# Two hybrid diffusion layers on one core: the feed-forward's GpSimd work moved to VectorE, modulation and sums of squares to TensorE

## The chip, the core and the metric

The kernel runs on one NeuronCore of a Trainium2 chip. The core has a matmul engine (TensorE, PE in the views, its weight loads PEld), a vector engine (VectorE, DVE), an activation engine (ScalarE, ACT), a general engine (GpSimd, POOL) and a queue that issues the loads here (SyncE, SP). The metric is the device time of one execution in microseconds; less is better.

## What is computed

Two layers run on 512 latent tokens and 256 context tokens of width 1024. Each layer is a half-step SwiGLU feed-forward, a mixer of four head groups, and a second half-step SwiGLU. Every block is preceded by an RMS norm and a modulation whose shift, scale and gate come from a conditioning vector through a matrix of 1024 x 9216 per layer. The lines that matter here are these:

```python
def rms_norm(x, g):
    y = xf * lax.rsqrt(jnp.mean(xf * xf, -1, keepdims=True) + RMS_EPS)
def modulate(h, shift, scale):
    return h * (1.0 + scale) + shift
def swiglu(h, w_in, w_out):
    u = h @ w_in
    return (jax.nn.silu(u[..., :D_FF]) * u[..., D_FF:]) @ w_out
...
    mod = (jax.nn.silu(c) @ w_mod[l] + b_mod[l]).reshape(c.shape[0], N_MOD, 1, D_MODEL)
    mod_c = (jax.nn.silu(c_ctx) @ w_mod[l] + b_mod[l]).reshape(N_MOD, 1, D_MODEL)
    x = x + 0.5 * mod[:, 2] * swiglu(modulate(rms_norm(x, norm_g[l, 0]), mod[:, 0], mod[:, 1]), ffn_w_in[l, 0], ffn_w_out[l, 0])
```

D_FF is 2816, that is 22 blocks of 128. All data are float32. The last feed-forward runs on the latent tokens alone.

## The kernel before

**Stages.** The program is six stages in a row: feed-forward 1 of layer 0, mixer 0, feed-forward 2 of layer 0, feed-forward 1 of layer 1, mixer 1, feed-forward 2 of layer 1. They are called FF1, mixer, FF2, FF3, mixer, FF4 below. Activations are kept transposed, features on partitions: `xT` is eight tiles of 128 features x 768 tokens.

**One block of a feed-forward.** `up` makes the 128 gate and 128 value features of one block from seven products in place of eight: tokens are cut in two halves of 384 (256 in FF4), the 1024 input features in even and odd tiles of 128, and the products EVEN1, T1, T2, ODD1, T3, ODD2, T4 are taken of sums and differences of these, on the side of the tokens (made once per stage, by `pair_even` and `pair_odd`) and on the side of the weights (made per block, by `w1_operands`). Every operand is split in two fp32r parts, high and low: ScalarE writes the high part (L440), VectorE the low part (L441). A product is four pairs of feature tiles times three matmuls (high x high, high x low, low x high), so a block is 84 matmuls of 384 or 386 columns (`ul`, L484). Banks of PSUM carry running sums from product to product; ScalarE copies some out (`pc`), VectorE adds some (L489), and the next product on that bank waits for these.

After `up`, three multiplications with the tokens' 1/rms (`rsb`, L526), the bias columns `ub`, silu, the gating (L539) and another split (L543, L544) give the block's hidden features. Two or three blocks are a chunk (CK); after a chunk the down-projection `y` adds its share to `xT`: 8 output tiles x blocks x 3 matmuls x 2 token segments (L428, L430, L432), then one VectorE operation per segment (L563).

**GpSimd's part.** L455 makes four weight combinations of 128x512 per block on GpSimd (`w1s`, `w1r`), and two of the three multiplications with `rsb` (L526) are GpSimd's too. So are two differences per pair in `pair_odd` (L378, L382).

**Modulation.** A block of the modulation is 512 of its columns. Four blocks are made at the start by `mod_direct` (L203: eight float32 matmuls with 32 output rows each, into four column groups of the array; L205 copies the sums out, L208 turns them into columns). The other 32 (14 in FF1, 6 in FF2, 12 in FF3) are made in the background by `mod_block`: eight loads of 128x512, and VectorE multiplies and adds them one by one into `macc` (L225, L227), once per conditioning vector; `mod_sum` adds over partitions with small matmuls (L242, L248).

**Sums of squares.** For the next norm, ScalarE squares each `xT` tile (L270), VectorE adds the squares up in `ss` (L271), and six small matmuls sum over partitions at the end (L297).

**Order.** The program is written in Tile: a scheduler orders the instructions of each engine by priorities (order of writing, shifted by `high_priority`) and by what its own model finds ready; LATER = 300 puts background work last. Every engine, the load queue too, then runs in that fixed order.

## Time and profile before

| | us |
|---|---|
| median of three runs | 3644.53 |
| the three runs | 3642.72, 3644.53, 3649.85 |
| the profiled execution | 3636.23 |
| its span, first to last instruction | 3634.4 |
| FF1 (its start in front: 76.9) | 628.9 |
| FF2 / FF3 / FF4 | 543.9 / 566.8 / 397.5 |
| mixers | 722.2 / 597.5 |

Stages are stretches of the one profiled execution, cut at the first product of each feed-forward's second block and at the last down-projection. Busy times of TensorE count overlapping matmuls once. Idle time is what is left of a stretch. A line of the view of groups has the line of the kernel, engine, operation, tiles out<-in, form, count, then busy time and mean duration, then the idle time ahead of it on its engine and who ended it.

### The profile page before, as it was taken

What the parts mean: (1) busy time and instruction counts of PE and PEld (TensorE: products, weight loads), DVE (VectorE), ACT (ScalarE), POOL (GpSimd) and SP (SyncE); (2) the same over time, 40 slices, a digit from 0 to 9 for tenths busy, and PEclk for the clock granted to TensorE, in tenths of its full rate; (3) what the DMA queues carried; (4) which work ended last, traced back from release to release, by engine and by line L of the source; (5) the groups of instructions that cost most, each with busy time, mean ns of one, the idle gap of its engine ahead of it and who ended that gap; (6) DMA issues with size and microseconds to landing.
All of it is one profiled execution on the core that took longest, in us unless ns stands there. A gap on an engine that the chain in (4) does not pass through costs nothing. (4 is left out here: it accounts for less than half of the span.)

```text
span 3634.4 us, 59477 instructions
## 1 busy us (share of the span) xinstructions
PE 3304.8 (91%) x22788; PEld 2804.5 (77%) x22788; DVE 2680.1 (74%) x5306; ACT 1496.4 (41%) x3168; POOL 1010.8 (28%) x910
## 2 busy tenths in 40 slices
PE   6898998899998997999999799999999989978887
PEld 5787788787775665888998788989888766567886
DVE  7898888645548867777776887777555578687776
ACT  5232333322447743333334433333423567443443
POOL 2343333100003212434442424433000023143442
PEclk9999999999999998999999899999999989999999
DMA  6333333211100002232221333333212100132221
GB/s 208 110 99 100 112 105 105 62 44 45 41 14 1 11 22 88 85 93 85 87 81 42 113 102 114 104 99 113 61 47 54 31 1 15 39 90 90 82 90 58
DMA packets 332941, 267.69 MB, mean 74 GB/s; under 512 B 33748, under 2 KB 281712, under 8 KB 332656
## 3 DMA queue, kind: packets, MB, share of 16 engines
q1 hardware_dynamic: 332656, 263.89, 24.4%
q8 instruction: 179, 2.93, 0.3%
q14 instruction: 106, 0.87, 0.1%
HBM read 261.73 MB, written 2.10 MB: 73 GB/s over the span
## 5 line engine op out<-in xcount | busy, mean ns | idle before, releaser
L484 PE MATMUL ul<-bh,w1h 128*128 128x386 f32 (+3 forms) x2464 | 833.3, 338 | 115.0 <-DVE sg L489 66.0
L484 PE MATMUL ul<-bh,w1l 128*128 128x386 f32 (+3 forms) x2464 | 816.9, 332 | 1.1 <-DVE w1l L441 1.0
L484 PE MATMUL ul<-bl,w1h 128*128 128x386 f32 (+3 forms) x2464 | 816.3, 331 | 0.0
L484 PEld LDWEIGHTS ul<-bh,w1h 128*128 128x128 f32 x2464 | 478.9, 194 | 157.8 <-DVE sg L489 72.0
L440 ACT ACTIVATE w1h<-w1r 128x512 fp32r<-128x512 f32 x528 | 329.9, 631 | 546.2 <-PE ul L484 311.0
L441 DVE TENSOR_TENSOR w1l<-w1r,w1h 128x512 fp32r<-128x512 f32 x528 | 441.3, 839 | 82.6 <-ACT w1h L440 81.7
L484 PEld LDWEIGHTS ul<-bh,w1l 128*128 128x128 f32 x2464 | 477.9, 194 | 9.7 <-issue 6.9
L484 PEld LDWEIGHTS ul<-bl,w1h 128*128 128x128 f32 x2464 | 479.7, 195 | 3.1 <-issue 2.9
L227 DVE SCALAR_TENSOR_TENSOR macc<-wm,sc,macc 128x512 f32<-128x512 f32 x392 | 414.2, 1076 | 7.0 <-DMA wm<-in_w_mod_dram 6.6
L563 DVE SCALAR_TENSOR_TENSOR xT<-y,gate,xT 128x512 f32<-128x512 f32 x448 | 266.8, 630 | 167.2 <-PE y L432 166.8
L455 POOL TENSOR_TENSOR w1s<-w1r 128x512 f32<-128x512 f32 x88 | 137.1, 1558 | 908.3 <-DVE w1l L441 831.2
L432 PE MATMUL y<-gh,w2l 128*128 128x512 f32 x1232 | 349.7, 355 | 37.4 <-DVE w2l L441 37.3
L428 PE MATMUL y<-gh,w2h 128*128 128x512 f32 x1232 | 351.5, 355 | 13.0 <-ACT w2h L440 10.9
L430 PE MATMUL y<-gl,w2h 128*128 128x512 f32 x1232 | 347.4, 352 | 0.2 <-DVE gl L544 0.2
L455 POOL TENSOR_TENSOR w1r<-w1r 128x512 f32<-128x512 f32 x176 | 269.8, 1533 | 164.9 <-issue 108.1
L440 ACT ACTIVATE w2h<-wo 128x384 fp32r<-128x384 f32 (+1 forms) x256 | 124.3, 494 | 351.2 <-PE y L430 317.1
L432 PEld LDWEIGHTS y<-gh,w2l 128*128 128x128 f32 x1232 | 199.2, 193 | 78.3 <-DVE w2l L441 47.0
L428 PE MATMUL pj<-hh,pwh 128*128 128x512 f32 (+2 forms) x864 | 251.8, 342 | 3.3 <-DVE qA L1092 1.8
L432 PE MATMUL pj<-hh,pwl 128*128 128x512 f32 (+2 forms) x864 | 243.1, 336 | 1.5 <-DVE pwl L441 1.5
L430 PE MATMUL pj<-hl,pwh 128*128 128x512 f32 (+2 forms) x864 | 244.2, 337 | 0.0
L428 PEld LDWEIGHTS y<-gh,w2h 128*128 128x128 f32 x1232 | 201.7, 193 | 48.3 <-ACT w2h L440 15.5
L430 PEld LDWEIGHTS y<-gl,w2h 128*128 128x128 f32 x1232 | 199.9, 192 | 32.2 <-DVE gl L544 0.5
(383 smaller groups left out, 5628.7 us busy)
## 6 DMA issues: line engine op xcount, KB each, us to landing
w1r<-in_ffn_w_in_dram SPq DMA_DIRECT2D x352, 256.0 KB
wm<-in_w_mod_dram SPq DMA_DIRECT2D x288, 256.0 KB
wo<-in_ffn_w_out_dram SPq DMA_DIRECT2D x88, 512.0 KB
pw<-in_w_in_dram SPq DMA_DIRECT2D x46, 512.0 KB
pw<-in_w_in_dram SPq DMA_DIRECT2D x16, 256.0 KB
wo<-in_w_out_dram SPq DMA_DIRECT2D x128, 32.0 KB
wo<-in_w_out_dram SPq DMA_DIRECT2D x64, 64.0 KB
rtab<-in_k_rope_dram SPq DMA_DIRECT2D x4, 512.0 KB
```

Source lines behind the costliest of these rows:

```text
L227: eng.scalar_tensor_tensor(out=acc[v], in0=r, scalar=s, in1=acc[v], op0=ALU.mult, op1=ALU.add)
L428: nc.tensor.matmul(p, lhsT=wh, rhs=xh[:, o:o + n], start=first, stop=False)
L430: nc.tensor.matmul(p, lhsT=wh, rhs=xl[:, o:o + n], start=False, stop=False)
L432: nc.tensor.matmul(p, lhsT=wl, rhs=xh[:, o:o + n], start=False, stop=last)
L440: nc.scalar.activation(out=hi, in_=raw, func=AF.Copy)
L441: nc.vector.tensor_tensor(out=lo, in0=raw, in1=hi, op=ALU.subtract)
L455: tt = lambda out, x, y, op: nc.gpsimd.tensor_tensor(out=out, in0=x, in1=y, op=op)
L484: nc.tensor.matmul(out, lhsT=w[:, m, :], rhs=x[:, m, x0:], start=start and m == j == 0, stop=m == KT // 2 - 1 and j == 2, skip_group_check ...
L563: nc.vector.scalar_tensor_tensor(out=xs, in0=py[s], scalar=gt[s][:, n_:n_ + 1], in1=xs, op0=ALU.mult, op1=ALU.add)
```

## The change

The 32 background blocks of modulation are made by TensorE as at the start: `mod_load` loads half a block (four tiles `wm`, where two were kept), `mod_some` multiplies the half that is there (four float32 matmuls, 32 x 512, in four column groups) and loads the next; one half per feed-forward block, two while many are left. `mod_block` and `mod_sum` are gone, and with them L225, L227, L242 and L248.

The sums of squares are added by TensorE: six matmuls of one column (four where there are only latent tokens) for each of the eight tiles, into one bank; the additions L271 are gone.

GpSimd has nothing left in the feed-forwards: combinations, multiplications and differences are VectorE's, the two bias columns are ScalarE's.

`ready` makes the tokens' operands in the order in which the products take them: of each pair first EVEN1, T1 and T2, and the rest of all four pairs after the last tile, at lower priority (REST). At the start, the rest is made between the first block's products, and the weights of the first block are loaded ahead of two modulation blocks. The down-projection's weights of a chunk are loaded together, one block ahead of the chunk's last.

```diff
-    def mod_block(self, l, b):
-        for k in range(KT):
-            r = self.raw.tile([128, 512], F32, name="wm", tag="wm", bufs=2)
-            nc.sync.dma_start(out=r, in_=a["w_mod"][l, k * 128:(k + 1) * 128, b * 128:b * 128 + 512])
-            for v in vs:
-                s = self.sc[:, k, v:v + 1]
-                eng = nc.gpsimd if v and MODPOOL else nc.vector
-                if k == 0:
-                    eng.tensor_scalar(out=acc[v], in0=r, scalar1=s, scalar2=None, op0=ALU.mult)
-                else:
-                    eng.scalar_tensor_tensor(out=acc[v], in0=r, scalar=s, in1=acc[v], op0=ALU.mult, op1=ALU.add)
-        self.macc = l, b, vs, acc
...
-        pt = self.psum("modps", "ms")
-        for v in vs:
-            for h in range(2):
-                g = 2 * v + h
-                with self.tc.high_priority(offset=g):
-                    nc.tensor.matmul(pt[32 * g:32 * g + 32, :256], lhsT=self.ones1, rhs=acc[v][:, 256 * h:256 * h + 256], start=True, stop=True)
...
+    def mod_load(self):
+        self.mod_now = None
+        if self.mod_todo:
+            l, b, h = self.mod_now = self.mod_todo.pop(0)
+            self.mod_w = [self.raw.tile([128, 512], F32, name="wm", tag="wm", bufs=4) for _ in range(4)]
+            for k, r in enumerate(self.mod_w):
+                self.nc.sync.dma_start(out=r, in_=self.a["w_mod"][l, (4 * h + k) * 128:(4 * h + k + 1) * 128, b * 128:b * 128 + 512])
+    def mod_some(self, left):
+        nc = self.nc
+        for _ in range(2 if len(self.mod_todo) + 1 > left else 1):
+            if self.mod_now is None:
+                return
+            l, b, h = self.mod_now
+            if h == 0:
+                self.mod_ps = self.psum("modps", "ms")
+            for k, r in enumerate(self.mod_w):
+                with self.tc.high_priority(offset=k):
+                    nc.tensor.matmul(self.mod_ps[32 * k:32 * k + 32, :], lhsT=self.sc[:, 4 * h + k, :], rhs=r, start=h == 0, stop=h == 1,
+                                     skip_group_check=True)
+            if h == 1:
+                self.mod_rows(l, b, self.mod_ps)
+            self.mod_load()
...
-    def sumsq(self, k, segs=SEGS):
+    def sumsq(self, k, segs=SEGS, tag="ms"):
...
         n0, n1 = segs[0][0], segs[-1][0] + segs[-1][1]
         if k == 0:
-            self.ss = self.work.tile([128, T], F32, name="ss", tag="ss", bufs=1)
-            nc.scalar.activation(out=self.ss[:, n0:n1], in_=self.xT[k][:, n0:n1], func=AF.Square)
-            return
+            self.ssps = self.psum("ssps", tag)
         sq = self.work.tile([128, T], F32, name="sq", tag="t3")
         nc.scalar.activation(out=sq[:, n0:n1], in_=self.xT[k][:, n0:n1], func=AF.Square)
-        nc.vector.tensor_tensor(out=self.ss[:, n0:n1], in0=self.ss[:, n0:n1], in1=sq[:, n0:n1], op=ALU.add)
+        for b in range(n0 // 128, n1 // 128):
+            nc.tensor.matmul(self.ssps[:, b:b + 1], lhsT=sq[:, b * 128:(b + 1) * 128], rhs=self.mean, start=k == b == 0, stop=k == KT - 1,
+                             skip_group_check=True)
+        if k == KT - 1:
+            self.ss = self.work.tile([128, 8], F32, name="ssc", tag="ssc", bufs=1)[:, :n1 // 128]
+            nc.vector.tensor_copy(self.ss, self.ssps[:, :n1 // 128])
...
-    def pair_odd(self, m, segs, e2, o2, new):
+    def pair_odd(self, m, segs, e2, o2, t):
...
         ne, go = self.rg[-1][:, 2 * m:2 * m + 1], self.rg[0][:, 2 * m + 1:2 * m + 2]
         self.second(2 * m + 1, segs, o2)
         yield
-        t = new()
         nc.vector.scalar_tensor_tensor(out=t, in0=e, scalar=ne, in1=e2, op0=ALU.mult, op1=ALU.add)
         self.parts(T1, m, t)
         yield
-        nc.gpsimd.tensor_tensor(out=t, in0=o2, in1=t, op=ALU.subtract)
+        nc.vector.tensor_tensor(out=t, in0=o2, in1=t, op=ALU.subtract)
         self.parts(T2, m, t)
         yield
         self.parts(ODD1, m, o, go)
-        nc.gpsimd.tensor_tensor(out=e2, in0=o2, in1=e2, op=ALU.subtract)
+        yield
+        nc.vector.tensor_tensor(out=e2, in0=o2, in1=e2, op=ALU.subtract)
         self.parts(T3, m, e2)
         yield
         self.parts(ODD2, m, o2)
         self.parts(T4, m, t)
         yield
...
+                self.held, self.rest = [], []
+            with self.tc.high_priority(offset=-SQ1):
+                self.sumsq(k, segs, tag)
...
-            new = lambda tag="pc", bufs=NPC: self.tmp.tile([128, self.half], F32, name="x2", tag=tag, bufs=bufs)
+            m = k // 2
             if k % 2 == 0:
-                self.e2 = new("sg", 1)
-                self.pair_even(k // 2, segs, self.e2)
-            else:
-                for _ in self.pair_odd(k // 2, segs, self.e2, new(), new):
-                    pass
+                self.held.append([self.half_tile() for _ in range(3)])
+                self.pair_even(m, segs, self.held[m][0])
+                return
+            e2, o2, t = self.held[m]
+            self.rest.append(self.pair_odd(m, segs, e2, o2, t))
+            for _ in range(3):
+                next(self.rest[m])
+            if k == KT - 1:
+                for i in range(3):
+                    with self.tc.high_priority(offset=-REST - 15 * i):
+                        for c in self.rest:
+                            next(c)
...
-        tt = lambda out, x, y, op: nc.gpsimd.tensor_tensor(out=out, in0=x, in1=y, op=op)
+        tt = lambda out, x, y, op: nc.vector.tensor_tensor(out=out, in0=x, in1=y, op=op)
         yield cut(q[0, 0])
...
             wh, wl = next(ops)
+            if first and n != EVEN1:
+                for r in self.rest:
+                    next(r, None)
...
+        self.mod_todo = [(*t, h) for t in background for h in range(2)]
...
-            wo = self.raw.tile([128, cn, D], F32, name="wo", tag="wo", bufs=1)
...
-                nc.sync.dma_start(out=wo[:, j, :], in_=w2[l, i, ff * 128:(ff + 1) * 128, :])
...
                 mul(nc.vector, g[:, :H], p[:, 2:H + 2], self.rsb[:, :H])
-                mul(nc.gpsimd, g[:, H:], g[:, H:], self.rsb[:, H:])
-                mul(nc.gpsimd, t[:, 2:], t[:, 2:], self.rsb)
+                mul(nc.vector, g[:, H:], g[:, H:], self.rsb[:, H:])
+                mul(nc.vector, t[:, 2:], t[:, 2:], self.rsb)
...
-                    nc.vector.tensor_copy(b[:, 0, :], t[:, 0:2])
-                    nc.vector.tensor_copy(b[:, 1, :], p[:, 0:2])
+                    nc.scalar.copy(b[:, 0, :], t[:, 0:2])
+                    nc.scalar.copy(b[:, 1, :], p[:, 0:2])
...
-                self.mod_sum()
                 with self.tc.high_priority(offset=-LATER):
-                    background(ff)
+                    if ff:
+                        self.mod_some(DFF // 128 - ff)
+                    else:
+                        self.mod_load()
                 if ff < DFF // 128 - 1:
                     ahead = self.up(l, i, ff + 1, False)
+                if j == cn - 2:
+                    wo = self.raw.tile([128, cn, D], F32, name="wo", tag="wo", bufs=1)
+                    for q in range(cn):
+                        nc.sync.dma_start(out=wo[:, q, :], in_=w2[l, i, (f + q) * 128:(f + q + 1) * 128, :])
...
+            if ci == len(chunks) - 1:
+                if switch:
+                    switch()
+                else:
+                    self.held_open([(self.fw, "pc", NPC, 1), (self.fw, "sg", 1, 2), (self.raw, "wm", 4, 1), (self.work, "ss", 1, 2)])
...
         for b in (8, 12):
-            self.mod_direct(0, b, ring(self.hl, "w1h", 4, NW1) + ring(self.hl, "w1l", 4, NW1))
+            self.mod_direct(0, b, self.mod_pieces(0, b, ring(self.hl, "w1h", 4, NW1) + ring(self.hl, "w1l", 4, NW1)))
+        self.first_w1 = self.w1_load(0, 0, 0)
...
-        for _ in range(5):
-            for s in stages:
-                next(s)
-        for k in range(KT):
-            self.sumsq(k)
-        self.raw_rows(self.fw)
-        with self.tc.high_priority(offset=-SOON):
-            for b in (0, 4):
-                w = self.raw.tile([128, 6, 512], F32, name="wm6", tag="wo", bufs=1)
-                self.mod_direct(0, b, [w[:, i, :] for i in range(6)] + ring(self.raw, "wm", 2, 2))
+            t = self.fw.tile([128, self.half], F32, name="x2", tag="pc", bufs=NPC)
+            self.pair_even(m, SEGS, x2[:, 0, :])
+            self.rest.append(self.pair_odd(m, SEGS, x2[:, 0, :], x2[:, 1, :], t))
+        for c in self.rest:
+            next(c)
+        with self.tc.high_priority(offset=-SQ0):
+            for k in range(KT):
+                self.sumsq(k)
+            self.raw_rows(self.fw)
```

What moves on the engines is shown at three places. On VectorE, in FF1 between the hidden features of two blocks, before:

```order
L227 SCALAR_TENSOR_TENSOR macc_2949<-wm,sc,macc_2949 128x512
L227 SCALAR_TENSOR_TENSOR macc_2950<-wm,sc,macc_2950 128x512
L489 TENSOR_TENSOR sg<-ul,pc 128x384
L441 TENSOR_TENSOR w1l<-w1s,w1h 128x512
L227 SCALAR_TENSOR_TENSOR macc_2949<-wm,sc,macc_2949 128x512
L489 TENSOR_TENSOR u_2798<-ul,pc 128x384
L441 TENSOR_TENSOR w1l<-w1r,w1h 128x512
L227 SCALAR_TENSOR_TENSOR macc_2950<-wm,sc,macc_2950 128x512
```

The same place after the change:

```order
L511 TENSOR_TENSOR sg<-ul,pc 128x384
L456 TENSOR_TENSOR w1l<-w1r,w1h 128x512
L549 TENSOR_TENSOR sg<-sg,rsb 128x384
L456 TENSOR_TENSOR w1l<-w1r,w1h 128x512
L474 TENSOR_TENSOR w1s<-w1r 128x512
L549 TENSOR_TENSOR sg<-ul,rsb 128x384
L456 TENSOR_TENSOR w1l<-w1r,w1h 128x512 x2
```

The modulation's `macc` rows are gone from between the additions and splits, and combinations (L474) and multiplications (L549) that GpSimd made stand there.

On TensorE, in FF1, a background block's matmuls before, between the last product of one block and the first of the next:

```order
L484 MATMUL ul<-bl_129,w1h 128x386
L484 MATMUL ul<-bh_128,w1l 128x386
L242 MATMUL modps<-macc_1519,ones_144 32x256 x2
L242 MATMUL modps<-macc_1520,ones_144 32x256 x2
L484 MATMUL ul<-bh_116,w1h 128x386
L484 MATMUL ul<-bl_117,w1h 128x386
L484 MATMUL ul<-bh_116,w1l 128x386
L248 MATMUL modpt<-pick,mrow 128x4 x2
```

A block's matmuls after, in the down-projection of FF1's third chunk:

```order
L445 MATMUL y<-gl,w2h 128x256
L447 MATMUL y<-gh,w2l 128x512
L447 MATMUL y<-gh,w2l 128x256
L241 MATMUL modps<-wm,sc 32x512 x8
L216 MATMUL modpt<-pick,mrow 128x2 x4
L443 MATMUL y<-gh,w2h 128x512
```

Both halves of a block stand in one row of eight there, so the second half's loads, which take the same four tiles, lie between its matmuls. The two halves stand so at six of the 32 blocks: four in FF1 and two in FF3. Elsewhere other matmuls lie between them.

On VectorE at the end of the first mixer, where the last output projection (L1423, in the changed kernel L1458) adds to `xT` tile by tile and FF2's token operands are made, before:

```order
L1423 SCALAR_TENSOR_TENSOR xT_77<-op,gate_6282,xT_77 128x512
L352 SCALAR_TENSOR_TENSOR bl_13410<-xT_76,gs_13431,bh_13409 128x384
L271 TENSOR_TENSOR ss<-ss,sq 128x768
L349 TENSOR_TENSOR bl_13406<-x_13587,bh_13405 128x384
L349 TENSOR_TENSOR bl_13412<-x_13565,bh_13411 128x384
L349 TENSOR_TENSOR bl_13414<-x_13584,bh_13413 128x384
L1423 SCALAR_TENSOR_TENSOR xT_77<-op,gate_6284,xT_77 128x256
```

After:

```order
L1458 SCALAR_TENSOR_TENSOR xT_77<-op,gate_6192,xT_77 128x512
L344 TENSOR_TENSOR bl_13309<-x_13477,bh_13308 128x384
L1458 SCALAR_TENSOR_TENSOR xT_77<-op,gate_6194,xT_77 128x256
L372 TENSOR_TENSOR x_13477<-x_13476,x_13477 128x384
L347 SCALAR_TENSOR_TENSOR bl_13307<-xT_77,gs_13334,bh_13306 128x384
L1458 SCALAR_TENSOR_TENSOR xT_78<-op,gate_6192,xT_78 128x512
```

Fewer operations stand between two additions to `xT`; the later products' operands have moved behind the last of them. Ahead of FF2's first product, all 48 matmuls of the squares stand in one row on TensorE, behind the last matmul of the projection.

## Rows read from the trace of the kernel before

**Rows 1.** The page's part 1: busy time, share of span, instructions, by engine.

```profile
PE 3304.8 (91%) x22788; PEld 2804.5 (77%) x22788; DVE 2680.1 (74%) x5306; ACT 1496.4 (41%) x3168; POOL 1010.8 (28%) x910
```

**Rows 2.** View by stretches: from:to length, PE PEld DVE ACT POOL busy (count), clock, DMA.

```profile
76.90:705.80 628.90, 559.98 (x3013) 501.46 (x3011) 547.40 (x818) 204.44 (x378) 207.81 (x128) 0.95 0.34 102
...
1455.00:1998.90 543.90, 517.32 (x2895) 480.94 (x2893) 412.63 (x661) 206.20 (x387) 205.51 (x130) 0.98 0.26 79
...
2034.00:2600.80 566.80, 533.59 (x2936) 489.54 (x2934) 448.80 (x693) 202.01 (x373) 195.00 (x128) 0.98 0.34 101
...
3213.50:3611.00 397.50, 350.12 (x2290) 316.22 (x2290) 299.28 (x444) 167.74 (x325) 164.96 (x126) 0.96 0.26 78
```

**Rows 3.** The same view of unstalled stretches: products, a down-projection, FF4's products, FF4's down-projection.

```profile
1585.31:1615.10 29.79, 29.79 (x171) 29.79 (x170) 18.77 (x31) 13.08 (x25) 16.26 (x11) 1.00 0.34 101
1507.83:1533.42 25.59, 25.59 (x146) 22.21 (x146) 16.36 (x28) 5.77 (x10) 3.66 (x3) 1.00 0.20 62
3204.26:3207.20 2.94, 2.94 (x26) 2.94 (x26) 2.94 (x7) 2.13 (x5) 0.99 (x3) 1.00 0.83 219
3252.63:3271.47 18.84, 16.80 (x73) 13.20 (x72) 12.60 (x19) 5.44 (x10) 3.50 (x4) 1.00 0.19 55
```

**Rows 4.** TensorE's waits in FF1: who waited for whom, us, times, longest us.

```profile
PE ul L484 <- DVE sg L489: 27.2, 13, 2.8
PE modps L242 <- DVE macc L227: 16.1, 8, 3.9
PE ul L484 <- ACT pc L492: 14.2, 12, 1.8
PE y L432 <- DVE w2l L441: 10.7, 7, 4.0
```

**Rows 5.** Two lines' durations in the program (ns, least/median/most), then VectorE groups in FF1.

```profile
L441 DVE TENSOR_TENSOR w1l<-w1r,w1h x528: 673/683/2050, 30.3 to 3585.7; 128x512 fp32r<-128x512 f32 x176
...
L455 POOL TENSOR_TENSOR w1r<-w1r x176: 1267/1622/1965, 34.8 to 3582.4; 128x512 f32<-128x512 f32 x176
...
L227 DVE SCALAR_TENSOR_TENSOR macc<-wm,sc,macc 128x512 f32<-128x512 f32 x195 | 205.6, 1078 | 1.4 <-DMA wm<-in_w_mod_dram 1.2
L441 DVE TENSOR_TENSOR w1l<-w1r,w1h 128x512 fp32r<-128x512 f32 x125 | 105.1, 841 | 8.3 <-ACT w1h L440 8.1
...
L539 DVE SCALAR_TENSOR_TENSOR sg<-u,ub,sg 128x512 f32<-128x512 f32 x21 | 33.2, 1580 | 2.0 <-ACT sg L537 2.0
```

**Rows 6.** Small matmuls: the start's in order of time, then FF1's groups.

```profile
20.17 4.10 PE L203 MATMUL modps<-wm,sc 128*32 128x512 f32 x16
...
24.95 1.05 PE L208 MATMUL modpt<-pick,mrow 128*128 128x2 f32 x8 [0.68 <-ACT mrow L205]
...
33.40 1.47 PE L297 MATMUL ssps<-mean,ss 128*128 128x1 f32 x12 [0.41 <-DVE gs L258]
...
L242 PE MATMUL modps<-macc,ones 128*32 128x256 f32 x112 | 18.3, 476 | 16.1 <-DVE macc L227 16.1
L248 PE MATMUL modpt<-pick,mrow 128*128 128x4 f32 x56 | 7.7, 243 | 0.0
```

**Rows 7.** Order of time: one load's issue and its reader; the output projection, freely running.

```profile
0.74 0.39 SPq L138 DMA_DIRECT2D ident<-in_k_ident_dram  x1
...
3.21 0.18 PEld L153 LDWEIGHTS colps<-ident,stage 16*128 16x128 f32 x1 [3.21 <-DMA ident<-in_k_ident_dram]
...
1385.44 12.20 PE L1420 MATMUL op<-kv,wo 128*128 128x512 f32 x36
```

**Rows 8.** View by stretches: FF1's last chunk, then the three ways into FF2, FF3, FF4.

```profile
667.80:705.80 38.00, 29.80 (x146) 24.65 (x144) 29.70 (x51) 19.43 (x33) 1.69 (x4) 0.87 0.17 45
...
1385.40:1455.00 69.60, 47.06 (x172) 34.60 (x172) 63.86 (x111) 35.16 (x74) 22.93 (x17) 0.80 0.33 99
1963.80:2034.00 70.20, 52.81 (x254) 44.75 (x253) 59.61 (x109) 39.22 (x80) 25.66 (x19) 0.83 0.22 68
3169.60:3213.50 43.90, 30.22 (x134) 20.78 (x132) 39.61 (x87) 25.92 (x63) 16.94 (x17) 0.84 0.38 114
```

More of the change, by code (lines that the diff above doesn't have):

```diff
@@ L294, in rstd @@
         n = (segs[-1][0] + segs[-1][1]) // 128
[L295 to L298 removed]
+        return self.rsqrt(self.ss, n, RMS_EPS)
     def halves(self):
```

104 lines of the change are left out of this document (48 added, 56 removed).

## The prediction

> **What bounds the kernel now.** I read the shares by engine first [rows 1]: TensorE 91% busy, VectorE 74%, GpSimd 28%. An average over stages decides nothing, so I cut the span into stages [rows 2] and asked of each what TensorE would need alone. An unstalled run of two blocks' products, 168 matmuls, takes 29.79 us, 14.9 a block; a down-projection of three blocks 25.59, 8.53 a block [rows 3]. From one cut to the next a feed-forward is 21 blocks of products and 22 of down-projection: 21 x 14.9 + 22 x 8.53 = 501 us (FF1's stretch has 21 further matmuls, 504). FF4 has 25 matmuls in 2.94 us, 9.9 a block, and 16.8 us busy for three blocks of down-projection, 5.6 a block [rows 3]: 21 x 9.9 + 22 x 5.6 = 331.
>
> The excess is 125 us in FF1, 43 in FF2, 66 in FF3, 67 in FF4 [rows 2]. Part of it is idle TensorE: 628.9 - 560.0 = 69, then 27, 33 and 47. Part is the granted clock, 0.95, 0.98, 0.98 and 0.96 of full, some 31, 11, 11 and 16 us of stretch lost. The rest is the modulation's small matmuls. TensorE's waits name VectorE and its neighbours [rows 4]: in FF1 27.2 us for the additions `sg`, 16.1 for `macc`, 10.7 for `w2l`, 14.2 for ScalarE's `pc`. VectorE is 87% busy there and 75 to 79% elsewhere, in fixed order, and its operations are long when GpSimd is at work: a split `w1l` takes 683 ns in the median but 841 in FF1's mean and up to 2050, the gating 1580 [rows 5]. So the feed-forwards are TensorE's, with stalls that VectorE makes.
>
> **VectorE's load.** FF1 loses L227 (205.6 us) and L225 (14 blocks, two each, under 20), some 222 in all. GpSimd's 207.8 us come over; the same 128x512 operation has a median of 683 ns on VectorE and 1622 on GpSimd [rows 5], a factor of 0.42, so 87 us. Contention with GpSimd goes: 125 splits x 158 ns and 21 gatings x some 840 ns, 38 us. VectorE: 547 - 222 + 87 - 38 = 374 us of some 590, 63% where it was 87%. FF2 and FF3 give, by the same factors (6 and 12 blocks of 16 us leave), some 366 and 320 us, 69% and 57%. FF4 has no modulation to lose: 299 + 69 from GpSimd less some 33 of contention is 335 us against 331 of TensorE. There VectorE is nearly full.
>
> **Stalls.** The `macc` waits go whole. The others are waits behind a long operation in VectorE's queue, or behind ScalarE standing on GpSimd or VectorE. With a shorter queue I let a third stay in FF1 to FF3 and half in FF4: idle falls from 69 to 18, 27 to 10, 33 to 9, 47 to 25, together -114 us. Bounds: nothing stays (-176), or FF1 comes to FF2's share of 5% and the rest stay (-38). The clock follows the idle; of 69 us lost I take back 28 (none to all).
>
> **Modulation on TensorE.** At the start eight such matmuls, 16 records, took 4.10 us at most, paced by their loads [rows 6]. Four column groups side by side would cost two waves of two passes; a float32 pass of 512 columns takes 0.41 us in the freely running projection (36 records, 24 of 512 and 12 of 256 columns, in 12.20 us) [rows 7], so 1.6 us. I take 2.0, nearer to the waves. The turn into columns is 1.05 us, with 0.68 us of wait for ScalarE's copy [rows 6] where it follows at once; I count half. That is 3.4 us a block (2.7 to 5.8), 109 for 32, less what goes, (18.3 + 7.7) / 14 = 1.86 us a block [rows 6] or 60: +49 (+27 to +126). The Trainium skill, "TensorE: Matmul & The Clock Gate", Part 3, says that matmuls in different column groups run at the same time, the span being one matmul's and a few ns for each more; by it a block is 1.6 us plus the turn, the term +36 and the time 13 us less.
>
> **Reloads.** Where both halves of a block stand in one row on TensorE, the second waits for four loads that could only be issued when the first had been multiplied. A load of 64 KB reached its reader 2.5 us after its issue [rows 7], and the start's matmuls drew their 256 KB loads at 0.68 us each (four of them in 2.7 us): 5.2 us. Six blocks stand so, 31 us; TensorE would partly have waited there for the hidden features anyway, so I count half, +15 (0 to 31).
>
> **Sums of squares.** 12 records, six matmuls, take 1.47 us [rows 6], so 48 take 11.8, 10.3 more than now, in each last chunk. FF1's is 38.0 us for 25.6 of down-projection because VectorE needs it [rows 8]; there the squares fill time that VectorE gives back. I count +20 for the chunks ahead of the two mixers (0 to 40).
>
> **Ways into FF2, FF3 and FF4.** Today these take 69.6, 70.2 and 43.9 us, VectorE 85 to 92% busy [rows 8], TensorE's work being about 20.6 + 14.9, 25.6 + 14.9 and 14 + 9.9. After the change five VectorE operations of a pair, where there were nine, lie between the additions to `xT`, some 6 us a pair in place of 12; but the squares stand behind the last projection, and the deferred operands still precede the first low weights. I take 55, 56 and 39: -34 (-70 to +10). The start reorders the same work behind the same loads: -5.
>
> **Sum.** 49 - 114 - 28 + 15 + 20 - 34 - 5 = -97 us. The profiled execution was 3636.2, so 3539; the runs' median is 8.3 higher, so 3548. The mixers are unchanged.
>
> **The rivals.**
> 1. More comes back: all idle and clock loss of FF1 to FF3 vanish, and the ways into the stages shorten by 60. For it: VectorE falls below 70% in all three. Against it: products still wait for additions on the same bank. About -185: 3460.
> 2. Only FF1 gains. VectorE near full in FF4 and the modulation's 3.4 us a block eat what FF2 and FF3 win: -38, squares and ways cancelling: 3607.
> 3. Slower, by reloads: TensorE's order is fixed, and a half's loads are issued only when the four tiles are free, behind the weight loads in the queue. If halves that now have other matmuls between them wait too, at 5.2 us each, the other terms' -112 are gone after 21 halves; with 40 of 64 halves waiting, 3644 - 112 + 208 = 3740. Against it: at 26 of the 32 blocks ten or more matmuls lie between.
> 4. Slower, by adding to the fullest engine: no idle comes back, and TensorE carries +49 of modulation, +65 of squares (304 matmuls of 0.245 less 9) and +15: 3644 + 129 = 3773. For it: TensorE is the busiest engine [rows 1]. Against it: the waits in [rows 4] are VectorE's. The Trainium skill, "Perfetto Trace Analysis", Identifying the Most-Contended Engine, would have the engine of the highest occupancy made lighter first, TensorE being judged by its weight loads; those are busy 77%, VectorE 74%, so the rule speaks against this change; the stage rows do not bear it out.
>
> **How the numbers follow.** My forecast has 0.55, with a range of its own from 3500 to 3600; rival 1 0.20, rival 2 0.13, rival 3 0.07, rival 4 0.05. Faster means below 3637 and slower above 3652; 0.2% is about what a measurement of this kernel can tell. Rival 2 lies near enough to give 0.03 to no change. So 0.86 faster, 0.03 same, 0.11 slower. The terms' ends, taken as independent, reach some 90 us below and 125 above; the range goes from rival 1 to past rival 2, 3460 to 3635.
>
> **What would show it.** GpSimd idle in the feed-forwards; `w1l` near 683 ns in the mean; VectorE at 60 to 70% in FF1 to FF3 and about 90% in FF4; FF1 near 600 us, FF2 near 530, FF3 near 570, FF4 near 375. Wrong would be: TensorE waits for `wm` loads of over 50 us, FF3 longer than before by over 10 us, or a low clock through the rows of squares. If FF1's idle stays above 40 us, the stalls were not VectorE's queue.

## The result, and the profile after

The changed kernel takes 3584.44 us (median of four runs, 3578.53 to 3594.11) against 3643.62 before, a ratio of 0.984 (95% interval 0.981 to 0.987). The forecast was 3548, with 3500 to 3600 as its own range: the direction is right, and 59 of the 97 us came.

The page's shares by engine after, to be read beside [rows 1]:

```profile
PE 3417.7 (95%) x23736; PEld 2892.2 (81%) x23736; DVE 2365.4 (66%) x5210; ACT 1533.6 (43%) x3342; POOL 163.9 (5%) x342
```

GpSimd and VectorE are relieved as planned, and TensorE is busy 113 us longer than before in a span that is 50 us shorter. The view by stretches after: from:to length, busy time (and count) of PE, PEld, DVE, ACT, POOL, then the clock. The stretches are FF1 from its first product on, its last chunk, the way into FF2, FF2, the way into FF3, FF3, the way into FF4, and FF4.

```profile
69.60:689.80 620.20, 594.00 (x3343) 515.89 (x3342) 402.45 (x726) 227.73 (x451) 1.00 (x2) 0.99 0.36 111
647.50:689.80 42.30, 38.08 (x229) 30.73 (x227) 30.01 (x58) 20.05 (x37) 0.00 (x0) 1.00 0.46 141
1386.50:1444.60 58.10, 58.10 (x260) 47.80 (x259) 47.71 (x105) 34.70 (x75) 0.00 (x0) 0.82 0.32 105
1444.60:1968.50 523.90, 520.16 (x2991) 480.85 (x2990) 378.45 (x658) 214.16 (x430) 0.00 (x0) 1.00 0.27 85
1937.20:2002.90 65.70, 60.69 (x339) 56.04 (x337) 52.49 (x108) 39.53 (x82) 0.00 (x0) 0.84 0.21 65
2002.90:2572.80 569.90, 554.62 (x3128) 492.53 (x3128) 377.78 (x657) 210.47 (x412) 1.02 (x2) 0.98 0.33 103
3164.00:3204.80 40.80, 38.07 (x190) 29.82 (x188) 37.29 (x97) 26.88 (x66) 0.00 (x0) 0.83 0.41 127
3204.80:3570.10 365.30, 352.27 (x2378) 320.55 (x2377) 291.18 (x523) 174.04 (x371) 0.00 (x0) 0.99 0.28 85
```

Against [rows 2], TensorE's idle time falls from 69, 27, 33 and 47 us to 26, 4, 15 and 13; VectorE's share from 87, 76, 79 and 75% to 65, 72, 66 and 80%. FF1's stretch before began at its second block; from its first product on it was 649.1 us, with 68 us idle and VectorE 87% busy as well. FF4's stretch in [rows 2] stops 8.7 us short of its last down-projection; up to that it was 406.2 us, 49 of them idle. So FF2 is 20 us shorter, FF3 3 us longer and FF4 41 shorter. Start and FF1, up to the last down-projection, take 689.8 in place of 705.1. TensorE's waits in the whole program after: who waited for whom, us, times, longest. Rows of the mixers are left out.

```profile
...
PE modpt L216 <- ACT mrow L213: 18.3, 25, 1.1
PE modps L241 <- DMA wm<-in_w_mod_dram: 17.5, 7, 3.1
PE ssps L265 <- ACT sq L263: 14.3, 3, 12.2
...
PE ul L506 <- DVE sg L511: 3.1, 4, 1.6
...
PE ul L506 <- ACT pc L517: 1.2, 1, 1.2
```

Of the waits of [rows 4], those for `macc` and `w2l` are gone, and 3.1 and 1.2 us are left of the other two. What TensorE waits for outside the mixers is now mostly the new work: the modulation's copies and loads, and the squares.

**The modulation.** TensorE in FF3 after, in order of time (start, us, what): a block with both its halves in one row.

```profile
2045.04 1.07 PE L241 MATMUL modps<-wm,sc 128*32 128x512 f32 x8
2048.84 3.88 PE L241 MATMUL modps<-wm,sc 128*32 128x512 f32 x8 [2.74 <-DMA wm<-in_w_mod_dram]
2053.40 1.05 PE L216 MATMUL modpt<-pick,mrow 128*128 128x2 f32 x8 [0.68 <-ACT mrow L213]
```

Four matmuls, half a block, take 1.07 us, 2.1 a block. Where the second half follows at once it waits for loads, and the block takes 7.7 us from its first matmul to its last product.

**The squares.** The same view at the end of the first mixer: the last output projection, the 48 small matmuls, half a block of modulation, FF2's first products. Behind it, from the view by stretches for the tile `ssps`, the row ahead of the first mixer.

```profile
1386.54 20.80 PE L1455 MATMUL op<-kv,wo 128*128 128x512 f32 x64
1407.18 17.99 PE L265 MATMUL ssps<-mean,sq 128*128 128x1 f32 x96
1425.10 1.91 PE L241 MATMUL modps<-wm,sc 128*32 128x512 f32 x2
1426.94 0.69 PE L506 MATMUL ul<-bh,w1h 128*128 128x386 f32 x1
1427.43 0.53 PE L506 MATMUL ul<-bl,w1h 128*128 128x386 f32 x1
```

```profile
689.80:703.60 13.80, 13.80 (x79) 13.66 (x78) 0.00 (x0) 0.62 0.03 10
```

The squares take 18.0 us here, not 11.8, and 13.8 ahead of the first mixer, where nothing hides them. The granted clock is 0.62 of full in the mean of the row ahead of the mixer. The view by stretches for the end of that row, all instructions:

```profile
694.00:703.60 9.60, 9.60 (x47) 9.58 (x46) 0.00 (x0) 1.86 (x3) 0.38 (x1) 0.50 0.04 14
```

In the last 9.6 us the granted clock stands at 0.50, the lower of its two levels (1.2 GHz), and a record of a square takes 0.20 us. The prediction's 1.47 us for 12 records are 0.12 a record. Ahead of FF2 the first products behind the squares start 0.32 us apart, at a granted clock of 0.50 too, where later ones start 0.175 apart.

### The profile page after: what moved, and what is told of

It is laid out like the page before. It is cut to its first block, busy times and chain, and to the rows that moved or that the text cites. A ratio compares the mean times of both kernels' runs of the same rounds, so it can differ in the third digit from the quotient of the medians.

```text
span 3584.3 us, 60380 instructions
## 1 busy us (share of the span) xinstructions
PE 3417.7 (95%) x23736; PEld 2892.2 (81%) x23736; DVE 2365.4 (66%) x5210; ACT 1533.6 (43%) x3342; POOL 163.9 (5%) x342
## 5 line engine op out<-in xcount | busy, mean ns | idle before, releaser
L506 PE MATMUL ul<-bh,w1h 128*128 128x386 f32 (+3 forms) x2464 | 807.5, 328 | 11.0 <-ACT w1h L455 4.1
L506 PE MATMUL ul<-bh,w1l 128*128 128x386 f32 (+3 forms) x2464 | 800.4, 326 | 2.0 <-DVE w1l L456 2.0
L506 PE MATMUL ul<-bl,w1h 128*128 128x386 f32 (+3 forms) x2464 | 802.1, 326 | 0.0
L455 ACT ACTIVATE w1h<-w1r 128x512 fp32r<-128x512 f32 x528 | 328.3, 631 | 499.8 <-PE ul L506 435.3
L456 DVE TENSOR_TENSOR w1l<-w1r,w1h 128x512 fp32r<-128x512 f32 x528 | 359.8, 688 | 187.2 <-ACT w1h L455 182.6
L443 PE MATMUL y<-gh,w2h 128*128 128x512 f32 (+1 forms) x1232 | 348.6, 351 | 6.9 <-ACT gh L566 6.9
L445 PE MATMUL y<-gl,w2h 128*128 128x512 f32 (+1 forms) x1232 | 349.6, 349 | 0.3 <-DVE gl L567 0.2
L447 PE MATMUL y<-gh,w2l 128*128 128x512 f32 (+1 forms) x1232 | 347.2, 348 | 0.5 <-DVE w2l L456 0.4
L455 ACT ACTIVATE w2h<-wo 128x384 fp32r<-128x384 f32 (+1 forms) x256 | 124.7, 495 | 339.8 <-PE y L445 300.3
L443 PEld LDWEIGHTS pj<-hh,pwh 128*128 128x128 f32 x864 | 150.2, 196 | 27.5 <-issue 7.9
L447 PEld LDWEIGHTS pj<-hh,pwl 128*128 128x128 f32 x864 | 146.7, 195 | 19.6 <-issue 5.1
L445 PEld LDWEIGHTS pj<-hl,pwh 128*128 128x128 f32 x864 | 147.7, 196 | 18.1 <-issue 7.6
```

The lines of the kernel that those rows point to most:

```text
L443: nc.tensor.matmul(p, lhsT=wh, rhs=xh[:, o:o + n], start=first, stop=False)
L445: nc.tensor.matmul(p, lhsT=wh, rhs=xl[:, o:o + n], start=False, stop=False)
L447: nc.tensor.matmul(p, lhsT=wl, rhs=xh[:, o:o + n], start=False, stop=last)
L455: nc.scalar.activation(out=hi, in_=raw, func=AF.Copy)
L456: nc.vector.tensor_tensor(out=lo, in0=raw, in1=hi, op=ALU.subtract)
L506: nc.tensor.matmul(out, lhsT=w[:, m, :], rhs=x[:, m, x0:], start=start and m == j == 0, stop=m == KT // 2 - 1 and j == 2, skip_group_check ...
```

## The experiments

Two theories stood against each other. **A**: VectorE had too much to do; the modulation's leaving it removed the stalls, and TensorE paid for that. **B**: GpSimd had to stop; modulation and squares could have stayed on VectorE, and moving them is a loss. Times are medians; the kernel before stood at 3644 to 3647 beside these runs.

### One part undone: squares, modulation, GpSimd, squares and modulation

The squares, back on VectorE:

```diff
-        for b in range(n0 // 128, n1 // 128):
-            nc.tensor.matmul(self.ssps[:, b:b + 1], lhsT=sq[:, b * 128:(b + 1) * 128], rhs=self.mean, ...
...
+        nc.vector.tensor_tensor(out=self.ss[:, n0:n1], in0=self.ss[:, n0:n1], in1=sq[:, n0:n1], op=ALU.add)
```

> The changed kernel with one part undone: VectorE adds the squares up again, seven additions of 128x768 (or x512) per norm, and six (four) small matmuls sum over partitions at the end; priorities of this work stay as changed. Theory A (the squares' rows of small matmuls stand in TensorE's way: 13.8 us and 13.2 us ahead of the two mixers, 18.0, 11.5 and 10.5 us ahead of FF2, FF3 and FF4, and the clock is low behind each): 40 to 60 us less than the changed kernel's 3584, about 3535, the rows ahead of the mixers gone and the granted clock there above 0.8. Theory B (TensorE would be waiting there for VectorE anyway, the squares only fill the wait): 3584 within 8, and the idle time ahead of the first products grows by as much as the rows shrink.

3543.31 us, 0.972 (0.970 to 0.974) of before: 41 less than the changed kernel. Both theories of that text hold in a part of the program. TensorE in order of time, at the first mixer's begin and ahead of FF2:

```profile
682.95 0.51 PE L447 MATMUL y<-gh,w2l 128*128 128x512 f32 x2
683.39 0.25 PE L639 MATMUL colps<-ident,stage 36*128 36x36 f32 x1
683.57 0.62 PE L443 MATMUL pj<-hh,pwh 128*128 128x512 f32 x2
...
1405.90 2.72 PE L292 MATMUL ssps<-mean,ss 128*128 128x1 f32 x12 [20.24 <-DVE ss L266]
```

Ahead of the mixers the 13 to 14 us are gone each time. Ahead of FF2 a wait of 20.24 us stands where the squares stood: there the squares only filled a wait. These additions kept the changed kernel's low priority, which is the likely reason; no run varies it alone.

The modulation, back on VectorE:

```diff
-                    nc.tensor.matmul(self.mod_ps[32 * k:32 * k + 32, :], lhsT=self.sc[:, 4 * h + k, :], rhs=r, ...
...
+                    nc.vector.scalar_tensor_tensor(out=acc[v], in0=r, scalar=s, in1=acc[v], op0=ALU.mult, op1=ALU.add)
```

> The changed kernel with one part undone: the 32 background blocks of modulation are VectorE's again (16 operations of 128x512 per block, the loads in two buffers), the squares stay on TensorE and GpSimd stays out. TensorE loses 3.4 us of wide small matmuls a block and 1.1 us of turn plus its waits, and gets the partition sums back, about 1.9 us a block. Theory A (the move was worth it, because VectorE would be full): VectorE in FF1 is at some 402 + 210 us of work, more than the 615 us of the stretch, so FF1 comes to 640 and FF3 to 585, FF2 to 525, together 3584 + 35 = about 3620. Theory B (what GpSimd left was enough to free VectorE, and the modulation on TensorE is a net loss): FF1 585, FF2 510, FF3 545, together some 3515.

3474.01 us, 0.953 (0.951 to 0.955): 110 less than the changed kernel. Theory A is wrong by 146 us, on the wrong side, and theory B's 3515 is still 41 too high. FF1 and FF3 in the view by stretches:

```profile
69.50:652.70 583.20, 567.23 (x3183) 514.44 (x3182) 526.55 (x950) 222.63 (x452) 1.07 (x2) 0.98 0.39 119
...
1933.20:2472.20 539.00, 536.52 (x3055) 499.45 (x3055) 462.81 (x812) 216.78 (x429) 1.02 (x2) 0.99 0.37 113
```

VectorE is busy 90% of FF1, more than the 87% of before, and TensorE idles 16 us of 583 where it idled 69 of 629. A nearly full VectorE hardly stalls TensorE here.

GpSimd's work, back on GpSimd:

```diff
-        tt = lambda out, x, y, op: nc.vector.tensor_tensor(out=out, in0=x, in1=y, op=op)
+        tt = lambda out, x, y, op: nc.gpsimd.tensor_tensor(out=out, in0=x, in1=y, op=op)
```

and likewise two multiplications and the differences; the bias columns are VectorE's again.

> The changed kernel with one part undone: GpSimd makes the weight combinations, two of the three multiplications with the tokens' 1/rms and the differences of the token operands again, VectorE the two bias columns. Theory A (VectorE at 55 to 72 percent in the feed-forwards after the change has room for or without these, so what gave the stalls back is the modulation's leaving VectorE): 3584 within 15, w1l's mean back above 780 ns, TensorE's idle in the feed-forwards under 20 us each. Theory B (GpSimd's slow operations and the shared port were the stalls): idle of TensorE comes back by 25 us a stage, 3584 + 80 = about 3665.

3685.68 us, 1.011 (1.009 to 1.013): 101 more than the changed kernel and slower than before; theory B's 3665 is the nearer. FF1 by stretch, VectorE's group of `w1l` (count, then busy and mean ns), and TensorE's waits in the whole program, in this kernel and then in the kernel before:

```profile
72.00:722.70 650.70, 611.43 (x3343) 520.70 (x3342) 356.53 (x633) 221.25 (x409) 192.04 (x137) 0.97 0.34 106
```

```profile
L456 DVE TENSOR_TENSOR w1l<-w1r,w1h 128x512 fp32r<-128x512 f32 x528 | 426.4, 811 | 266.5 <-ACT w1h L455 259.6 <-PE modps L206 4.2 <-PE ul L506 2.1
```

```profile
PE ul L506 <- DVE sg L511: 24.0, 20, 2.0
...
PE ul L506 <- ACT pc L514: 14.3, 11, 2.9
```

```profile
PE ul L484 <- DVE sg L489: 66.0, 35, 3.7
...
PE ul L484 <- ACT pc L492: 36.0, 28, 3.0
```

VectorE is busy only 55% of FF1, and a part of the stalls is back. TensorE's idle time in the four feed-forwards, each from its first product to its last down-projection, is 122 us, where the changed kernel has 62 and the kernel before 192. So VectorE's share was not their cause. Idle time is 60 of the 101 us; TensorE's own busy time grows too, in FF1 from 594 to 611 us for as many matmuls, at a granted clock of 0.97 in place of 0.99.

Squares and modulation both back on VectorE, by the two edits above:

> The changed kernel with modulation and squares both VectorE's again; what is left of the change is that GpSimd is out of the feed-forwards, the order of the token operands and of the loads. Theory A (TensorE's relief needs the modulation off VectorE): VectorE is full in FF1 (402 + 210 us), about 3620 - 50 = 3570, FF1 no faster than 630. Theory B (taking GpSimd out is the whole gain): about 3515 - 50 = 3465.

3459.46 us, 0.948 (0.947 to 0.950), 6 from theory B's number and 110 from A's. The two moves to TensorE cost 3584.4 - 3459.5 = 125 us together; 184 come from the rest of the change.

### One part alone

The kernel before, with GpSimd's feed-forward work moved:

```diff
-                mul(nc.gpsimd, g[:, H:], g[:, H:], self.rsb[:, H:])
-                mul(nc.gpsimd, t[:, 2:], t[:, 2:], self.rsb)
+                mul(nc.vector, g[:, H:], g[:, H:], self.rsb[:, H:])
+                mul(nc.vector, t[:, 2:], t[:, 2:], self.rsb)
```

and likewise the combinations (L455) and differences (L378, L382); as in the change, the bias columns go to ScalarE.

> The kernel before with one part of the change alone: GpSimd's weight combinations, two multiplications with the tokens' 1/rms and the differences go to VectorE, the bias columns to ScalarE. Modulation and squares stay VectorE's, the order of token operands and loads stays. Theory A (taking GpSimd out is the whole gain, because every VectorE operation gets shorter: 1076 ns to 745 for a multiply-add of the modulation, 839 to 685 for w1l): within 30 of the 3459 of the changed kernel with modulation and squares back on VectorE. Theory B (the order of operands and loads carries a good part): 3500 to 3580.

3445.83 us, 0.945 (0.943 to 0.947): about 200 less than before, and below the kernel with squares and modulation back. So the new order of operands and loads, which that kernel has and this one lacks, gave nothing. FF1 by stretch, then the modulation's multiply-add by line (least, median, most in ns), first in this kernel, then in the kernel before:

```profile
71.70:639.00 567.30, 553.41 (x3127) 506.95 (x3126) 519.06 (x925) 215.77 (x436) 1.28 (x3) 0.98 0.40 119
```

```profile
L227 DVE SCALAR_TENSOR_TENSOR macc<-wm,sc,macc x392: 739/746/779, 98.1 to 2368.0; 128x512 f32<-128x512 f32 x196
```

```profile
L227 DVE SCALAR_TENSOR_TENSOR macc<-wm,sc,macc x392: 735/744/2034, 74.8 to 2507.3; 128x512 f32<-128x512 f32 x196
```

The median never changed. The mean was 1076 ns in the program before and 747 here: close to a third of it came with GpSimd's work.

The modulation alone moved to TensorE, in the kernel before (`mod_some` in place of `mod_block`, as in the change):

> The kernel before with one part of the change alone: the background modulation goes to TensorE (half a block at a time, four load buffers); GpSimd keeps its work, squares and order stay. It tells whether the move pays while GpSimd makes VectorE slow. Theory A (it does: 3643 less VectorE's 414 us of multiply-adds, FF1 falls by 30): 3600 to 3630. Theory B (TensorE's price of about 110 outweighs it in every case): 3660 to 3700; the changed kernel with GpSimd back stands at 3686 with 41 of squares in it, which speaks for 3645.

3660.01 us, 1.003 (1.001 to 1.006), a little slower than before, at the lower end of theory B's range. FF1 is 637.8 us from its first product on, 649.1 before, but the first product begins at 87.2, not 56.0. VectorE in FF1 is busy 53%. Below it is TensorE's longest wait at the start:

```profile
87.20:725.00 637.80, 603.60 (x3296) 515.06 (x3295) 339.15 (x615) 215.17 (x394) 183.69 (x131) 0.98 0.34 105
```

```profile
PE ssps L290 <- DVE ss L264: 36.8, 1, 36.8
```

The late start, 31 us, is a wait for VectorE's additions of squares, which the move was not meant to touch; why they come so late there stays open. The four feed-forwards are 19 us shorter together. So with GpSimd at work the move gives back at least about what it costs, and this run doesn't tell more; without GpSimd it costs 84 (both back against squares back) to 110.

Only the four weight combinations moved, in the kernel before; then all but the differences moved:

> The kernel before with only the four weight combinations of a block moved from GpSimd to VectorE; the multiplications with the tokens' 1/rms and the differences stay GpSimd's. About two thirds of GpSimd's time in the feed-forwards goes. Theory A (GpSimd's work costs by its time at work, through every VectorE operation beside it): two thirds of the 198 us between the kernel before and the kernel with all of GpSimd's work moved, so 3644 - 130 = about 3515. Theory B (it costs where something on the way of a block waits for it, and that is the multiplications): 3600 or more.

> As the kernel before with all of GpSimd's feed-forward work moved (3446), but the differences of the token operands stay GpSimd's; they run at the start and on the ways into FF2 to FF4 only. With them on VectorE the first product began at 71.7 us in place of 56.0, behind a wait of 27 us for the norm's rows. Theory A (VectorE is the one that is late there): the first product before 62, and 3446 less 5 to 20. Theory B (GpSimd's slow differences are as late, and slow VectorE down): 3446 within 5, or more.

3489.20 us, 0.958 (0.956 to 0.960), and 3437.33, 0.944 (0.941 to 0.947). The combinations alone are 156 of the 200 us, more than the two thirds of theory A, whose 3515 is still the nearer; with the multiplications left on GpSimd the multiply-add still takes 908 ns:

```profile
L227 DVE SCALAR_TENSOR_TENSOR macc<-wm,sc,macc 128x512 f32<-128x512 f32 x392 | 349.6, 908 | 5.4 <-DMA wm<-in_w_mod_dram 4.8
```

With the differences left on GpSimd the first product begins at 58.1 us, not 71.7, as theory A had it. The 8.5 us between the medians are of the size that the intervals leave open; this is the fastest kernel of the study, 5.6% below before.

### What GpSimd does to VectorE

To tell contention from waits for slow results, GpSimd got work that nobody reads, in the kernel with squares and modulation back:

```diff
+                nc.gpsimd.tensor_tensor(out=scr, in0=self.ident, in1=b[:, 0, 0:1].to_broadcast([128, 128]), op=ALU.add)
+                for _ in range(21):
+                    nc.gpsimd.tensor_tensor(out=scr, in0=self.ident, in1=self.ident, op=ALU.add)
```

> The changed kernel with modulation and squares back on VectorE (3459), and in each block of a feed-forward 22 additions of 128x128 on GpSimd whose sums nobody reads, some 10 us a block, as much as GpSimd had before the change; only the first of a block waits for something (the block's bias columns). Theory A (GpSimd's work slows VectorE's operations by itself, whoever waits for it): w1l's mean rises from 685 ns to 780 or more, the modulation's multiply-add from 745 to 950 or more, and the time rises by 60 to 200. Theory B (what cost the time was that products and gatings waited for GpSimd's slow results): w1l within 20 ns of 685, the time within 15 of 3459.

3596.10 us, 0.987 (0.984 to 0.990): 137 more than without it, for nothing. The first two of VectorE's groups without the additions (the kernel with both back), then its groups with them:

```profile
L472 DVE TENSOR_TENSOR w1l<-w1r,w1h 128x512 fp32r<-128x512 f32 x528 | 356.7, 685 | 49.8 <-ACT w1h L471 43.1 <-PE modps L206 4.5 <-PE ul L522 0.3
L237 DVE SCALAR_TENSOR_TENSOR macc<-wm,sc,macc 128x512 f32<-128x512 f32 x392 | 283.3, 745 | 6.5 <-DMA wm<-in_w_mod_dram 5.7
```

```profile
L472 DVE TENSOR_TENSOR w1l<-w1r,w1h 128x512 fp32r<-128x512 f32 x528 | 416.3, 799 | 39.6 <-ACT w1h L471 34.0 <-PE modps L206 5.1
L237 DVE SCALAR_TENSOR_TENSOR macc<-wm,sc,macc 128x512 f32<-128x512 f32 x392 | 310.5, 814 | 4.6 <-DMA wm<-in_w_mod_dram 4.4
L612 DVE SCALAR_TENSOR_TENSOR xT<-y,gate,xT 128x512 f32<-128x512 f32 x256 | 190.5, 744 | 72.9 <-PE y L463 72.0
```

The multiply-add rose less than theory A expected (814, not 950), but the price is contention's: nobody waits for `scr`. GpSimd is busy 1376 us here and 1011 in the kernel before, so the 137 us don't tell how much of the 200 was contention and how much were waits for its results. The last row does not move: `y` is in PSUM. In the kernel before it is the same, where operations with an input from PSUM never grew (by line, least, median, most):

```profile
L563 DVE SCALAR_TENSOR_TENSOR xT<-y,gate,xT x448: 466/739/753, 151.0 to 3619.8; 128x512 f32<-128x512 f32 x86, 128x256 f32<-128x256 f32 x64
...
L489 DVE TENSOR_TENSOR u<-ul,pc x176: 410/546/561, 71.6 to 3588.9; 128x384 f32<-128x384 f32 x67, 128x386 f32<-128x386 f32 x65, 128x258 f32<-128x258 f32 x22, 128x256 f32<-128x256 f32 x22
```

So the last test let GpSimd write without reading:

```diff
-                for _ in range(21):
-                    nc.gpsimd.tensor_tensor(out=scr, in0=self.ident, in1=self.ident, op=ALU.add)
+                for _ in range(50):
+                    nc.gpsimd.memset(scr, 0.0)
```

> As the kernel with GpSimd's unread additions (3596), but of the 22 additions of a block only the first, which waits for the bias columns, is left, and 50 fills of 128x128 with zero stand in the others' place: GpSimd writes as much and more, and reads next to nothing. Theory A (VectorE's operations are blocked by GpSimd's reads: those of VectorE with both inputs in SBUF came to 799 ns for w1l and 814 for the multiply-add, those with an input from PSUM stayed at 744 to 749 and 548 to 553): w1l within 20 ns of 685, the multiply-add within 20 of 745, the time within 15 of 3459. The Trainium skill, SBUF, State Buffer, Who interferes with whom, says that a VectorE instruction with two SBUF inputs contends with a GpSimd instruction that reads SBUF and not with one that only writes it. Theory B (any GpSimd work beside it slows VectorE, by its time at work): w1l above 750 and 3500 or more.

3448.64 us, 0.948 (0.945 to 0.951), as fast as without any of it. VectorE's first two groups, and GpSimd's:

```profile
L472 DVE TENSOR_TENSOR w1l<-w1r,w1h 128x512 fp32r<-128x512 f32 x528 | 357.7, 687 | 45.4 <-ACT w1h L471 39.1 <-PE modps L206 4.5
L237 DVE SCALAR_TENSOR_TENSOR macc<-wm,sc,macc 128x512 f32<-128x512 f32 x392 | 284.9, 750 | 8.3 <-DMA wm<-in_w_mod_dram 7.3 <-DVE w2l L472 0.4
```

```profile
L587 POOL MEMSET scr<- 128x128 f32 x4400 | 913.8, 208 | 252.6
```

GpSimd is busy 914 us with fills and VectorE does not notice. It is GpSimd's reading of SBUF that holds up VectorE's operations with two inputs there. The Trainium skill, "SBUF — State Buffer", Who interferes with whom, says just that, and calls the contention an exclusive lock; the trace agrees, with 2034 ns at most for a multiply-add of 735 beside GpSimd operations of 1267 to 1965.

The trace of the kernel before also shows how. Of its 392 multiply-adds 136 took more than 800 ns. 135 of these began while a GpSimd operation was running, and every one of the 135 ended 544 to 553 ns after that operation did. The other way round nothing happens to VectorE: 90 times a GpSimd operation began while one of the other 256 multiply-adds was at work, and none of the 256 took more than 753 ns. So an operation of VectorE that comes second waits until GpSimd's has ended, and long GpSimd operations cost it more than short ones: among the unread additions, 631 ns long in the mean, the longest multiply-add took 897 ns, where 2034 was the longest before.

### Column groups

```diff
-nc.tensor.matmul(self.mod_ps[32 * k:32 * k + 32, :], lhsT=self.sc[:, 4 * h + k, :], rhs=r, start=h == 0, stop=h == 1,
+nc.tensor.matmul(self.mod_ps[32 * (k % 2):32 * (k % 2) + 32, :], lhsT=self.sc[:, 4 * h + k, :], rhs=r, start=h == 0 and k < 2, stop=h == 1 and k >= 2,
```

> The changed kernel with the background modulation's matmuls in two column groups in place of four (64 output rows in place of 128). In the changed kernel eight matmuls, 16 records, take 3.4 us, where two waves of four side by side would take 1.6 by the estimate made ahead and one after the other 6.5. Theory A (only neighbours overlap, the second pass of one with the first of the next, so two groups do as well as four): 3.4 us a block still, the time 3584 within 10. Theory B (four run side by side and something else takes the time): 5 us a block or more, the time up by 50 or more.

3628.40 us, 0.995 (0.993 to 0.997): 44 more than the changed kernel. Half a block in two groups:

```profile
227.14 1.91 PE L241 MATMUL modps<-wm,sc 128*32 128x512 f32 x8
```

1.91 us against 1.07 in four groups: four do run side by side, and theory A is wrong; theory B's 5 us and 50 us are too high. Wrong, too, was the 3.4 us a block that both theories began from: it was FF1's busy time of all modulation matmuls through 16, and that holds the start's late blocks and the rows stretched by late loads. A block is 2.1 us, or 3.8 in two groups.

## Why the prediction held, and where its steps failed

The time from the first product of a feed-forward to its last down-projection, in single profiles (us; the first line is when FF1's first product begins):

| | before | after | squares back | modulation back | GpSimd back | both back | GpSimd's part alone |
|---|---|---|---|---|---|---|---|
| begin of FF1 | 56.0 | 69.6 | 62.1 | 69.5 | 72.0 | 62.9 | 71.7 |
| FF1 | 649.1 | 620.1 | 621.4 | 583.2 | 650.6 | 581.8 | 567.3 |
| FF1's end to mixer 0 | 0.8 | 14.0 | 0.1 | 13.3 | 14.0 | 1.0 | 0.8 |
| FF2 | 568.1 | 541.5 | 540.0 | 530.0 | 554.4 | 528.7 | 537.3 |
| FF2's end to FF3 | 2.4 | 13.2 | 20.2 | 12.3 | 13.8 | 17.7 | 1.5 |
| FF3 | 599.6 | 591.2 | 586.4 | 539.0 | 600.1 | 543.6 | 556.1 |
| FF3's end to mixer 1 | 0.1 | 13.2 | 0.1 | 10.7 | 14.2 | 1.3 | 1.0 |
| FF4 | 421.6 | 380.9 | 380.2 | 374.3 | 425.6 | 389.2 | 374.4 |
| span | 3634.4 | 3584.3 | 3535.7 | 3474.9 | 3684.8 | 3464.5 | 3437.6 |

- **What bounds the kernel** was right: the feed-forwards are TensorE's, with stalls that came by way of VectorE.
- **VectorE's load** is the step that failed, though its sums came near in two stages (FF1 63% forecast, 65% measured; FF2 69 and 72%). It put the multiply-adds, 205.6 us of FF1 at 1078 ns [rows 5], down to the modulation alone, and counted contention for splits and gatings only, 38 us. But the multiply-adds were contended as well: 392 x (1076 - 747) = 129 us of the program were GpSimd's. FF1's sum hides this, since the multiply-adds leave together with their contention; the conclusion that they had to leave does not follow, and as the runs show, VectorE could have kept them. The rows for that were there: the line's median was 744 ns beside the mean of 1076, the same reading that the prediction made for `w1l`. In FF4, which has no modulation, the undercount shows bare: 335 us and a nearly full VectorE were forecast, with 33 of contention gone; 291 us and 80% were measured. So some 77 us went, of which 11 are the bias columns, now ScalarE's. FF3's 57% came out as 66% for another reason. Eight of its twelve blocks serve one conditioning vector only, so some 121 us of L225 and L227 leave there, not 12 x 16 = 192.
- **Stalls**: forecast -114 us of idle time, measured 178 - 58 = -120, with FF4 taken to its end. The size was right by luck, for the cause was not: what stalled TensorE is not how much VectorE had to do but how long each operation took. With VectorE 90% busy and GpSimd out the stalls stay away; with VectorE 55% busy and GpSimd in a part of them comes back. The prediction's own sign, FF1's idle above or below 40 us, could not tell the two apart (it is 26), since the change took away the modulation and GpSimd together.
- **Modulation and reloads**: forecast +49 and +15, measured +110 by undoing it, or +84 with the squares on VectorE. The matmuls were forecast at 2.0 us a block and take 2.1. The turn takes 1.05 and, where it follows at once, a wait of some 0.8. The six blocks with both halves in one row take 7.7 to 9.1 us for their matmuls, 48.6 in all, in place of 6 x 2.1: 36 us of waiting where half of 31 was counted.
- **Squares**: forecast +20, measured +41 (+15 with the modulation on VectorE; 16 of the 26 us between these lie in FF4, and why stays open). The price of 0.12 us a record was that of a short row; in the long rows the clock falls, and a record takes up to 0.20. The rows ahead of the mixers are 14.0 and 13.2 us, and FF1's last chunk is 42.3 us, no shorter than the 38.0 of [rows 8]: three half-blocks of modulation, two turns and 24 matmuls of the last block's products stand in it now and fill what VectorE gave back, and the squares stand behind it.
- **Ways into the stages**: forecast -34, measured from the same places as in [rows 8] 58.1, 65.7 and 40.8 us, -19. The start came out 14 us later up to the first product, forecast 5 earlier: with the squares back on VectorE it is 7.5 earlier again, and the rest is not explained. In the kernel before, the differences on VectorE alone make it 13.6 later (71.7 against 58.1), but GpSimd's return does not undo it here (72.0).
- **Clock**: forecast 28 of 69 us back. By the same reckoning 0.99, 1.00, 0.98 and 0.99 leave 6, 0, 11 and 4 us lost, so some 48 came back. A low clock through the rows of squares was to be a sign of being wrong, and it came: 0.62 in the row ahead of the first mixer, 0.50 in its last 9.6 us.
- **The whole**: the terms overlap and can't be added up as measured. The start, the ways, the modulation and the squares each cost more than forecast, and the clock gave back more; that 3584 lies in the range owes something to these errors working against each other.

Rival 4, adding to the fullest engine, had its mechanism right: it said that what is added to TensorE is paid in full, and 125 us were paid where it had 129. That the two agree so well is luck: it had 64 for modulation and reloads, which cost 84 to 110, and 65 for the squares, which cost 15 to 41. Its forecast failed because the stalls went all the same. The Trainium skill, "Perfetto Trace Analysis", Identifying the Most-Contended Engine, was said not to be borne out here; for two of the change's parts it is, since moving work onto the engine with the highest occupancy lost, and moving work between the other engines won. What won, though, was work taken off GpSimd, the least busy engine at 28%.

## What to carry to other kernels

Before taking an engine's share as its load, compare the median of each costly line with its mean and its most: where the median is the undisturbed time and the mean is 40% above, another engine is inside that row, and its leaving can be worth more than moving the row's work away, as here. Price each part of a change with the other parts already in place; here one part was worth about 200 us, and the two that shared the credit cost 125. Here a VectorE that was 90% busy with short operations kept up, and one that was 55% busy with operations that sometimes took three times as long did not.

## What the runs showed of the hardware

- GpSimd operations that read SBUF lengthen VectorE operations with two SBUF inputs: 685 to 799 ns and 745 to 814 in the mean with unread additions beside them, up to 2034 for single ones in the kernel before. Those with an input from PSUM stay within 753 ns at the most, and GpSimd's fills, busy 914 us, lengthen nothing (687 and 750). The GpSimd operations that lengthened these have two inputs in SBUF; one with a single input was not run.
- In the kernel before, each of 135 lengthened multiply-adds began during a GpSimd operation and ended 544 to 553 ns after it; those that began first kept to 753 ns at most.
- Four float32 matmuls of 32 x 512 in four column groups take 1.07 us, in two groups 1.91.
- In rows of 80 to 96 records of one-column matmuls TensorE is busy throughout in the records, and yet the granted clock falls, to 0.62 in the mean and 0.50 at the end of the row ahead of the first mixer; a record takes 0.165 to 0.19 us in the mean of a row. Ahead of FF2 the first ten products behind them start 0.32 us apart instead of 0.175.
